# A list schedule with its own shift for each of 1150 pieces of work, 225 operations on another engine, and transfers modelled as loads and stores

## The chip, the cores and the metric

One core of a Trainium2 chip. The metric is the device time of one execution in microseconds (us); lower is better. The kernel before takes 780.31 us, the median of three runs (779.22 to 782.52).

## The reference

One layer of a streaming encoder on a sequence of 1024 rows and 1024 columns, all in fp32:

```python
h = rms_norm(x, norm_pre_g)
proj = h @ w_in                       # 1024 x 2976: sb_q, sb_k, sb_v, sb_g, c_q, c_kv, k_rope, mla_g
sb_o = stick_breaking_attention(...)  # 8 heads of 64: sigmoid and a suffix product over the past keys
sb_y = head_rms_norm(sb_o, ...) * silu(sb_g)
q    = rms_norm(c_q) @ w_uq           # 8 heads, low-rank q and kv, rotary part of 32
kv   = rms_norm(c_kv) @ w_ukv
mla_o = latent_attention(...)         # softmax over the visible chunks of 64
mla_y = head_rms_norm(mla_o, ...) * silu(mla_g)
y = concat(sb_y, mla_y) @ w_out
x = x + rms_norm(y, norm_post_g)
ple = rms_norm(p @ w_ple, ple_norm_g)
x = x + ple * sigmoid(x @ w_ple_gate + b_ple_gate)
```

## The kernel before

**Arithmetic.** A product of fp32 operands is made of three matmuls: each operand is split into a high part (`copy` to the type fp32r) and a low part (`tensor_tensor` subtract), and high x high, high x low and low x high are summed in PSUM. `split` makes the two parts; its `heng` and `leng` say on which engine. Tiles have 128 partitions and up to 512 columns; a PSUM bank is 128x512.

**Stages.** At the start the rows of `x` are loaded, normalised (`x_norm`), transposed on TensorE and split (`x_tr`), and multiplied by the columns of `w_in` for the values (`xv_gen`, 24 matmuls for each row tile). Then the two attentions run, 16 pairs (head pair, half of the queries), as `unit(i, s)`: load the head's queries and keys (`load_head`), scores and weights row block by row block (`sb_rows`, `mla_rows`), then transposes of the weights and the product with the values (`av`), then head norm and gate (`finish1` to `finish3`). Between them other projections are woven in as filler: queries and keys of later heads (`qk_gen`), the gates (`gate_gen`), the low-rank part (`c_gen`, `lr_*`), the per-layer embedding (`ple_gen`, around 400 to 480 us), and the output projection (`wo_gen`, `e1_gen`). The tail multiplies by `w_ple_gate` with a seven-product scheme (`wg_part`, `e2a`, `e2b`) and writes the output. Queries, keys, values, gates and other intermediate arrays go through DRAM (`q_d`, `k_d`, `v_d`, `gate_d`, `y_d`).

**What sets the order.** The program isn't issued as it is written. A `Recorder` takes every operation as a record with its dependences, a duration from `cost` and a priority; `schedule` then runs a list schedule over five queues (PE, ACT, DVE, POOL, and SP, which issues all transfers): of the operations that are ready on the queue that is free first, the one with the lowest priority number comes next. The priority is the number of the operation in the recorded order, plus `LOW` (336) for filler, minus `URGENT` or `AHEAD` in some places:

```python
prio=i + (LOW if self.low else 0) + self.bias
```

A tile of a pool gets its buffer in the recorded order of the tiles of that pool (`info["order"]`, `grant`): the pool `u` has 28 buffers for the main work, `f` has 10 for filler, PSUM has 3 banks `a` (sums of products) and 5 banks `t` (scores and transposes). `issue` then emits the operations sorted by their planned start, so every engine works through a fixed list. Since one line emits everything, all instructions have the same line in the profile (L517 here), and they are told apart by engine and by their tiles: `a` and `t` the PSUM banks, `u` and `f` the SBUF buffers, `h` the transposed input or later the large weights, names ending in `_d` DRAM arrays, names beginning with `in_` the inputs.

**Engines.** `choice(i)` puts the low part of a split or a product on DVE or POOL by the table `SPLITS`; high parts are on ACT or DVE by `heng`.

Of the kernel before, what the change touches and what calls it, by code (L numbers as in the profile page):

```python
# [52 lines left out]
LOW = 336  # L53
# [13 lines left out]
HEAD = ("v0", "x1", "x0", "g0", "v3", "v1", "v2", "x2")  # L67
AHEAD = 52
BANKS = {"a": ("a", 3), "t": ("t", 5), "s": ("t", 5), "v": ("a", 3), "l": ("t", 5)}


class Weaver:
# [13 lines left out]
    def _step(self):  # L86
        name, gen, low = self.queue[0]
        self.rec.low = low
# [5 lines left out]
        self.rec.low = False  # L94

    def spend(self, cost):
# [64 lines left out]
class Recorder:  # L161
# [3 lines left out]
    def __init__(self, nc):  # L165
        self.ins = []
        self.tiles = {}
        self.tags = {}
        self.access = {}
        self.low = False  # L170
        self.front = False
        self.bias = 0

        self.shadow = bacc.Bacc("TRN2", target_bir_lowering=False, num_devices=1)
        self.PE = Proxy(self, "PE", nc.tensor)
        self.ACT = Proxy(self, "ACT", nc.scalar)
        self.DVE = Proxy(self, "DVE", nc.vector)
        self.POOL = Proxy(self, "POOL", nc.gpsimd)
        self.SP = Proxy(self, "SP", nc.sync)

    def tile(self, pool, shape, dt, tag, slots, name, kind, part=None):
# [20 lines left out]
        return t  # L202

    def touch(self, ap, info):
# [10 lines left out]
    def add(self, eng, op, fn, args, kw):  # L215
        aps = [a for a in list(args) + [v for k, v in kw.items() if k != "accum_out"] if isinstance(a, bass.AP)]
        outs = [aps[0]]
        if kw.get("accum_out") is not None:
            outs.append(kw["accum_out"])
        i = len(self.ins)  # L220
        deps = {}
        uses = []
        spaces = []
        for is_w, group in ((False, aps[1:]), (True, outs)):
            for pos, ap in enumerate(group):
# [15 lines left out]
                else:  # L241
# [7 lines left out]
        func = kw.get("func", args[2] if len(args) > 2 and op == "activation" else None)  # L249
        self.ins.append(dict(port=port, eng=eng, op=op, fn=fn, args=args, kw=kw, deps=deps, uses=set(uses), dur=dur,  # L250
                             cols=self.columns(op, args) if eng == "PE" else 0,
                             prio=i + (LOW if self.low else 0) + self.bias, func=SETS.get(func) if op == "activation" else None))

# [11 lines left out]
    def cost(self, eng, op, args, kw, outs, aps, spaces):  # L265
        n = max(self.elems(a) for a in aps)
        ps = any(k == "psum" for _, k in spaces)
        if eng == "PE":
# [26 lines left out]
        run = min(self.run(a) for a in aps)  # L295
        total = self.elems(outs[0]) * outs[0].shape[0]
        return total / run * (7.0 + run * 4 * 0.0372) / 16 * 1.2

    def run(self, ap):
        info = self.tiles.get(ap.tensor.name)  # L300
        n = 1
        for stride, k in reversed(ap.ap[0 if info is None or info["kind"] == "dram" else 1:]):
# [9 lines left out]
           ("DVE", "POOL"): 156.0, ("DVE", "SP"): 120.0, ("POOL", "PE"): 180.0, ("POOL", "ACT"): 75.0,  # L312
           ("POOL", "DVE"): 65.0, ("POOL", "POOL"): 102.0, ("POOL", "SP"): 55.0, ("SP", "PE"): 1060.0,
           ("SP", "ACT"): 910.0, ("SP", "DVE"): 910.0, ("SP", "POOL"): 980.0, ("SP", "SP"): 910.0}

    def schedule(self):
        import heapq
        ins, LAT = self.ins, self.LAT
        n = len(ins)
        succ = [[] for _ in range(n)]  # L320
        need = [0] * n
# [24 lines left out]
        slot = {}  # L346
        dma_free = 0.0
        port_free = 0.0
        table = None
# [68 lines left out]
        while done < n:  # L418
# [101 lines left out]
def block_kernel(ctx, tc, x, p, positions, norm_pre_g, w_in, q_norm_g, w_uq, kv_norm_g, w_ukv,  # L520
# [245 lines left out]

    for item in HEAD:
        first(item)
    R.bias = -URGENT
    for n in range(2):  # L770
# [6 lines left out]
    x_norm(1)  # L777
    for t in range(4):
        for _ in xv_gen(t):
            pass  # L780
# [167 lines left out]
    def lr_load_gen():  # L948
        lr_load()
        yield 0.0  # L950

    for _ in qk0_gen(0):
        pass
    for dst, src in ((g_sb, sb_out_norm_g), (g_mla, mla_out_norm_g)):
# [255 lines left out]
    def unit(i, s):  # L1210
# [4 lines left out]
        g1 = sb_rows(i, s, rows) if c < 4 else mla_rows(i, s, rows, ess[c, s], e)  # L1215
        g2 = pending.pop(0) if pending else iter(())
        for cost in g1:
            yield cost
            run_later()
            for _ in range(s + 1):  # L1220
                yield next(g2, 0.0)
        yield from g2
        pending.append(av_unit(i, s, rows))
# [27 lines left out]
    def wg_part(i):  # L1251

        if i == 1:
            for nm in ("B11", "B21", "T1"):
                wg[nm] = []
            for k in range(4):
                raw, b12 = k4((128, 2, 512), F32, "wg_r"), k2(dt=F32, name="wg_b")
                SP.dma_start(raw, w2g[:, k::4, half[0]])
# [11 lines left out]
        for a, nm in enumerate((("T4", "T2") if i == 2 else ("T3", "B22"))):  # L1270
            wg[nm] = [(h_[:, k, a], l_[:, k, a]) for k in range(4)]
        for k in range(4):
            ra = k4((128, 2, 512), F32, "wg_r")
            SP.dma_start(ra, w2g[:, k::4, half[1]])
# [60 lines left out]
    def e2a(t):  # L1335
# [10 lines left out]
        def parts(nm, src, heng, leng):  # L1346
            h_, l_ = k2(name="ah"), k2(name="al")
            split(h_, l_, src, heng=heng, leng=leng)
            out_[nm] = (h_, l_)
        parts("A11", ps[0, 0], ACT, DVE)  # L1350
        f11, f21 = k2(dt=F32, name="f11"), k2(dt=F32, name="f21")
# [9 lines left out]
        DVE.tensor_tensor(s4, ps[0, 1], s2, ALU.subtract)  # L1361
        parts("S4", s4, ACT, choice(36))
        choice(37).tensor_tensor(f11, f11, f21, ALU.subtract)
        parts("S3", f11, ACT, choice(38))
# [17 lines left out]
    def e2b(t, order, last):  # L1382
# [19 lines left out]
        for i in order:  # L1402
            if i == 4 and last:
                for v in (slice(0, 256), slice(256, 512)):
                    close(1, 0, product(xs, 4, v), w, w, v, DVE)
                continue
            ps = product(xs, i)
            if i == 1:
# [40 lines left out]
    def prepare(u):  # L1449
# [10 lines left out]
        if u and c == 0 and s == 1:  # L1460
            weave.ensure("b1")
        load_head(i, s)

    prepare(0)
    for u, (i, s) in enumerate(units):
        load_v(i, s)
        if u + 1 < len(units):
# [8 lines left out]
    while pending:  # L1476
        for _ in pending.pop(0):
            pass
    for _ in range(5):
        run_later(True)  # L1480
    weave.drain()
    R.front = True
    for t in range(N1, 4):
        for _ in e1_gen(t):
            pass
    y_load(4)
    R.front = False
    weave.drain()
    firsts = 0
    for step in TAIL:  # L1490
        k, t = step[0], int(step[1])
        if k == "x":
# [11 lines left out]
        else:  # L1504
            R.front = True
            if t < 6:
                if t + 1 < NT:
                    y_load(t + 1)
                for _ in e1(t, True):
                    pass  # L1510
            else:
# [5 lines left out]
                for n in range(3):  # L1517
                    for g in both:
                        for cost in g:
                            if cost == 0.0:  # L1520
                                break
# [29 lines left out]
```

## Time and profile before

| | |
|---|---|
| median of three runs | 780.31 us (779.22 to 782.52) |
| the profiled execution | 780.85 us; span on the core 778.8 us |
| TensorE matmuls | 756.4 us busy (97%), 3912 instructions |
| VectorE (DVE) | 569.8 us (73%), 1041 |
| ScalarE (ACT) | 422.1 us (54%), 1001 |
| GpSimd (POOL) | 395.1 us (51%), 355 |
| DMA | 148.69 MB, mean 191 GB/s; 386 issues, all from SP |

Times in the profile are in us from the start of the span, durations of single instructions in ns. "PE" is TensorE's matmul, "PEld" its weight load, "SPq" the issue of a transfer. A row of the timeline gives start, length, engine, operation, tiles and, in brackets, the idle time of the engine before it and what ended that. Matmuls overlap in the pipeline, so their lengths don't add up; what counts for them is the distance from start to start.

### The profile page before, as it was taken

The numbers are of one execution on the slowest core, as the hardware profiler recorded it, in microseconds if no ns is written. First come the engines' busy times: TensorE is split into PE (matmuls) and PEld (weight loads), VectorE is DVE, ScalarE is ACT, GpSimd is POOL, SyncE is SP. The second block draws the span as 40 slices with busy tenths as digits, with TensorE's granted clock in tenths as the row PEclk, the third lists the DMA queues.
The fourth block names the chain that finished last, engine by engine and source line by source line (L and its number), as shares of the span: only waits on it lengthen the run. The fifth ranks groups of instructions, "written<-read, shape, count | busy, mean of one in ns | idle before, by whom it ended". The sixth has DMA issues, their size and how long they took to land.

```text
span 778.8 us, 11830 instructions
## 1 busy us (share of the span) xinstructions
PE 756.4 (97%) x3912; PEld 624.7 (80%) x3912; DVE 569.8 (73%) x1041; ACT 422.1 (54%) x1001; POOL 395.1 (51%) x355
## 2 busy tenths in 40 slices
PE   5999999999999999999999999999999999999996
PEld 3887879988888878888887787888888878878875
DVE  5784225389837869888997999987689879564755
ACT  5415224244526576667547676875967672444431
POOL 5654225102422258878877721323287025579975
PEclk9999999999999999999999999999999999999999
DMA  9544361168998636475455688597356377073331
GB/s 339 188 163 135 130 186 53 57 219 327 348 343 274 191 124 218 127 238 173 149 190 189 194 271 272 187 311 240 122 202 190 112 233 264 1 269 109 101 137 60
DMA packets 101966, 148.69 MB, mean 191 GB/s; under 512 B 7441, under 2 KB 55057, under 8 KB 101906
## 3 DMA queue, kind: packets, MB, share of 16 engines
q1 hardware_dynamic: 101906, 147.95, 56.7%
q8 instruction: 31, 0.51, 0.3%
q14 instruction: 29, 0.24, 0.1%
HBM read 101.26 MB, written 46.66 MB: 190 GB/s over the span
## 4 chain that ended last, share of the span: by engine, by line
PE 81%; DMA 6%; DVE 5%; POOL 4%; ACT 2%; issue 1%; SPq 1%; POOLq 0%; DVEq 0%; ACTq 0%
PE a L517 56%; PE t L517 24%; DVE u L517 3%; POOL u L517 2%; DMA u<-in_w_ple_gate_dram 2%; POOL h L517 1%; ACT u L517 1%; DMA u<-q_d 1%; DVE f L517 1%; DMA ple_d<-f 1%; DVE nm L517 1%; DMA q_d<-f 1%; DMA u<-in_norm_pre_g_dram 1%; SPq L517 1%; DMA f<-in_p_dram 1%
## 5 line engine op out<-in xcount | busy, mean ns | idle before, releaser
L517 POOL TENSOR_TENSOR u<-u,u 128x512 f32<-128x512 f32 (+18 forms) x171 | 241.1, 1426 | 116.9 <-DVE u L517 56.9
L517 PE MATMUL a<-h,f 128*128 128x512 f32 x864 | 241.0, 406 | 1.0 <-DVE f L517 0.8
L517 PEld LDWEIGHTS a<-h,f 128*128 128x128 f32 x864 | 155.8, 188 | 29.0 <-DVE f L517 1.5
L517 DVE TENSOR_TENSOR u<-t,u 128x512 fp32r<-128x512 f32 (+4 forms) x284 | 149.3, 555 | 29.6 <-ACT u L517 23.9
L517 PE MATMUL t<-u,u 128*128 128x512 f32 (+4 forms) x576 | 151.4, 368 | 1.0 <-DMA u<-q_d 0.9
L517 ACT CAST u<-t 128x512 fp32r<-128x512 f32 (+1 forms) x252 | 111.8, 490 | 65.0 <-PE t L517 46.2
L517 PE MATMUL a<-u,u 128*128 128x512 f32 (+2 forms) x522 | 133.1, 370 | 0.8 <-DVE f L517 0.3
L517 PE MATMUL t<-ident,u 128*128 128x128 f32 x792 | 125.3, 274 | 3.3 <-ACT u L517 1.7
L517 PEld LDWEIGHTS t<-u,u 128*128 128x128 f32 x576 | 103.0, 189 | 20.1 <-ACT u L517 2.8
L517 PEld LDWEIGHTS t<-ident,u 128*128 128x128 f32 x792 | 97.3, 141 | 23.1 <-ACT u L517 4.5
L517 ACT ACTIVATE u<-t 128x384 f32<-128x384 f32 (+5 forms) x208 | 91.2, 518 | 45.0 <-PE t L517 33.6
L517 PE MATMUL a<-h,u 128*128 128x512 f32 (+1 forms) x492 | 115.5, 390 | 0.0
L517 PEld LDWEIGHTS a<-u,u 128*128 128x128 f32 x522 | 92.8, 188 | 18.9 <-DVE u L517 1.3
L517 PEld LDWEIGHTS a<-h,u 128*128 128x128 f32 x492 | 90.5, 188 | 20.4
L517 DVE TENSOR_TENSOR_SCAN u<-u 128x64 f32<-128x64 f32 (+3 forms) x64 | 68.9, 1086 | 27.1 <-ACT u L517 24.3
L517 DVE TENSOR_TENSOR u<-a,u 64x512 f32<-64x512 f32 (+4 forms) x75 | 47.8, 651 | 40.6 <-PE a L517 18.5
L517 ACT ACTIVATE u<-t,nms 128x384 f32<-128x384 f32 (+4 forms) x96 | 55.1, 579 | 28.5 <-DVE nms L517 26.3
L517 ACT ACTIVATE f<-a 128x512 bf16<-128x512 f32 (+2 forms) x64 | 34.6, 542 | 59.0 <-PE a L517 58.2
L517 DVE TENSOR_TENSOR u<-u,u 128x512 fp32r<-128x512 f32 (+4 forms) x59 | 58.5, 1004 | 6.5 <-ACT u L517 3.6
L517 DVE TENSOR_TENSOR f<-a,f 128x512 f32<-128x512 f32 (+2 forms) x54 | 34.4, 644 | 32.9 <-ACT f L517 28.4
L517 POOL TENSOR_TENSOR u<-u 128x512 f32<-128x512 f32 (+8 forms) x34 | 39.4, 1173 | 35.7 <-ACT u L517 18.7
L517 DVE TENSOR_REDUCE nm<-t 128x1 f32<-128x384 f32 (+4 forms) x96 | 51.9, 547 | 3.5 <-PE t L517 2.7
(98 smaller groups left out, 768.3 us busy)
## 6 DMA issues: line engine op xcount, KB each, us to landing
u<-q_d SPq DMA_DIRECT2D x64, 256.0 KB, 4.5
u<-k_d SPq DMA_DIRECT2D x16, 512.0 KB, 6.2
u<-v_d SPq DMA_DIRECT2D x16, 512.0 KB, 5.5
u<-in_w_ple_gate_dram SPq DMA_DIRECT2D x16, 512.0 KB, 6.2
f<-in_w_in_dram SPq DMA_DIRECT2D x14, 512.0 KB, 4.3
v_d<-u SPq DMA_DIRECT2D x12, 512.0 KB, 3.4
f<-in_x_dram SPq DMA_DIRECT2D x9, 512.0 KB, 5.0
k_d<-u SPq DMA_DIRECT2D x9, 512.0 KB, 3.7
```

The source lines that it names most:

```text
L517: x["fn"](*[place(a) for a in x["args"]], **{k: place(a) for k, a in x["kw"].items()})
```

## The change

The list schedule, the operations recorded and their arithmetic stay. Four things change.

1. **A place of its own for each piece.** The recording is cut into 1146 numbered pieces (`piece`, called at each step of each generator). A table `SHIFT` gives a piece two numbers: the first is added to the priority of its operations, the second to the place of its tiles in the order in which buffers are handed out (`turn`). Pieces without an entry have no shift. The order of buffers is now sorted by this number.
2. **An engine of its own for 225 operations.** `FLIP` lists record numbers; `other` puts such an operation on the other engine: 126 copies from ACT to DVE (43 of them the high part of transposed attention weights, 128 to 512 columns out of PSUM), 23 copies from DVE to ACT, 58 two-operand products or differences from POOL to DVE (21 of them products of the stick-breaking weights), 18 from DVE to POOL. By engine: DVE 1041 to 1184 operations, ACT 831 to 728, POOL 349 to 309; PE and SP are unchanged.
3. **The planner's model of transfers.** A store is expected to start moving 0.5 us after its issue and a load 1.7 us after; descriptors in flight are limited to 1500; durations and the latencies after a transfer are other numbers.
4. **The planner's costs** of POOL operations and of matmuls on bf16 operands are other numbers.

```diff
+SHIFT = {
+    0: (-2123, -1458), 1: (-359, -1410), 2: (53, -217), 3: (-206, -329), 4: (46, -202), 5: (230, -104),
...
+FLIP = (
+    7, 13, 62, 88, 90, 108, 134, 144, 181, 183, 202, 234, 235, 264, 290, 307, 326, 386, 425, 432, 435, 438, 441, 444,
...
+            self.tiles[key].update(turn=self.turn(1), turn0=len(self.ins), chunk=self.chunk)
...
+    def turn(self, by=0):
+        return len(self.ins) + SHIFT.get(self.chunk, (0, 0))[by]
...
+        if i in FLIP:
+            eng, op, fn = self.other(eng, op)
...
-                             prio=i + (LOW if self.low else 0) + self.bias, func=SETS.get(func) if op == "activation" else None))
+                             chunk=self.chunk, prio=self.turn() + (LOW if self.low else 0) + self.bias, func=SETS.get(func) if op == "activation" else None))
+
+    def other(self, eng, op):
+
+        to = {("DVE", "tensor_tensor"): self.POOL, ("POOL", "tensor_tensor"): self.DVE,
+              ("ACT", "copy"): self.DVE, ("DVE", "tensor_copy"): self.ACT}[eng, op]
...
-                return max(60.0, n * 0.451)
+                return n * 0.305
...
-            return n * 2.105 + 148
...
+            ap = outs[0].ap
+            if int(ap[-1][0]) == 2:
+                return n * 2.76 + 107
+            return n * 1.76 + 135 if len(ap) > 2 and int(ap[-1][1]) == 2 else n * 2.217 + 84
...
+        for info in self.tags.values():
+            info["order"].sort(key=lambda key: self.tiles[key]["turn"])
...
-                free[e] = s + 430.0
-                dma_free = max(s + 1150.0, dma_free) + x["dur"]
+
+                while flight and flight[0][0] <= s:
+                    room -= heapq.heappop(flight)[1]
+                while flight and room + x["descs"] > 1500:
+                    t, k = heapq.heappop(flight)
+                    room -= k
+                    s = max(s, t)
+                free[e] = s + x["hold"]
+                dma_free = max(free[e] + x["lead"], dma_free) + x["dur"]
                 end = dma_free
+                heapq.heappush(flight, (end, x["descs"]))
+                room += x["descs"]
```

Nearly every row of every engine's list moves. Three places follow.

**The first transfers, on SP.** `u` buffers are filled from the weights `w_in`, from rows of `x`, and from the gain row `norm_pre_g`, which TensorE spreads over the partitions as its first work. Before, the gain row is fourth:

```order
L517 DMA u_0_115<-in_w_in_dram 128x2x512
L517 DMA u_3_121<-in_x_dram 128x1024
L517 DMA u_4_125<-in_x_dram 128x1024
L517 DMA u_6_127<-in_norm_pre_g_dram 1x1024
L517 DMA u_7_129<-in_w_in_dram 128x2x512
```

Now it is third, and the rows of `x` that come first are those that are transposed first:

```order
L730 DMA u_0_115<-in_w_in_dram 128x2x512
L730 DMA u_3_121<-in_x_dram 128x1024
L730 DMA u_12_125<-in_norm_pre_g_dram 1x1024
L730 DMA u_10_127<-in_x_dram 128x1024
L730 DMA u_7_129<-in_w_in_dram 128x2x512
```

The gain row has passed one row tile of `x`.

**The second head's queries, on SP, around 105 us.** `f` buffers hold query stores (to `q_d1`) and weights of the low-rank projection; `u` buffers receive the stored queries again. Before:

```order
L517 DMA f_4_924<-in_w_in_dram 128x2x416
L517 DMA q_d1_84<-f_3_931 256x1x512
L517 DMA u_23_957<-q_d1_84 128x512
L517 DMA u_23_957<-q_d1_84 128x1x512
L517 DMA u_18_970<-q_d1_84 128x512
L517 DMA u_18_970<-q_d1_84 128x1x512
L517 DMA f_0_979<-in_w_in_dram 128x2x416
L517 DMA q_d1_84<-f_7_965 256x1x512
```

Now:

```order
L730 DMA f_4_927<-in_w_in_dram 128x2x416
L730 DMA q_d1_84<-f_6_939 256x1x512
L730 DMA f_0_958<-in_w_in_dram 128x2x416
L730 DMA q_d1_84<-f_3_956 256x1x512
L730 DMA u_20_975<-q_d1_84 128x512
L730 DMA u_20_975<-q_d1_84 128x1x512
L730 DMA u_1_986<-q_d1_84 128x512
L730 DMA u_1_986<-q_d1_84 128x1x512
```

The last weights and the second half of the queries no longer stand behind the four loads, which wait for the first store.

**The first embedding tile, on ACT, around 411 us.** The copies (`CAST`) of a `t` bank of 256 columns to an `f` buffer are the high parts of the transposed embeddings; the `ACTIVATE` rows are the sigmoids of stick-breaking scores and one of a gate (from an `a` bank). Before:

```order
L517 ACTIVATE f_4_3268<-a_1_290 128x512
L517 ACTIVATE u_23_3894<-t_1_180 128x512
L517 ACTIVATE u_8_3902<-t_1_180 128x512
L517 ACTIVATE u_23_3894<-t_4_249 128x512
L517 ACTIVATE u_8_3902<-t_4_249 128x512
L517 CAST f_0_3914<-t_0_164 128x256
L517 CAST f_0_3914<-t_3_198 128x256
L517 CAST u_27_3867<-t_4_249 128x128
```

Now:

```order
L730 ACTIVATE f_4_3481<-a_1_325 128x512
L730 CAST f_1_3894<-t_3_184 128x256
L730 CAST f_1_3894<-t_1_157 128x256
L730 ACTIVATE u_5_3901<-t_2_176 128x512
L730 ACTIVATE u_17_3909<-t_2_176 128x512
L730 ACTIVATE u_5_3901<-t_0_151 128x512
L730 ACTIVATE u_17_3909<-t_0_151 128x512
```

The two copies have passed the four sigmoids.

More of the change, by code (lines that the diff above doesn't have):

```diff
@@ L87, in _step @@
         name, gen, low = self.queue[0]
+        outer = self.rec.thread
+        self.rec.piece(name)
         self.rec.low = low
@@ L94, in _step @@
         self.rec.low = False
+        self.rec.piece(outer)
     def spend(self, cost):
@@ L249, in add @@
         func = kw.get("func", args[2] if len(args) > 2 and op == "activation" else None)
-        self.ins.append(dict(port=port, eng=eng, op=op, fn=fn, args=args, kw=kw, deps=deps, uses=set(uses), dur=dur,
+        back = any(int(st) < 0 for a in aps for st, _ in a.ap)
+        stored = eng == "SP" and spaces[-1][1] != "sbuf"
+        self.ins.append(dict(port=port, hold=525.0 if back else 420.0, descs=self.descriptors(aps, outs) if eng == "SP" else 0, lead=500.0 if stored else 1700.0, eng=eng, op=op, fn=fn, args=args, kw=kw, deps=deps, uses=set(uses), dur=dur,
                              cols=self.columns(op, args) if eng == "PE" else 0,
-                             prio=i + (LOW if self.low else 0) + self.bias, func=SETS.get(func) if op == "activation" else None))
+                             chunk=self.chunk, prio=self.turn() + (LOW if self.low else 0) + self.bias, func=SETS.get(func) if op == "activation" else None))
+    def other(self, eng, op):
+        to = {("DVE", "tensor_tensor"): self.POOL, ("POOL", "tensor_tensor"): self.DVE,
+              ("ACT", "copy"): self.DVE, ("DVE", "tensor_copy"): self.ACT}[eng, op]
+        op = {"copy": "tensor_copy", "tensor_copy": "copy"}.get(op, op)
+        return to.name, op, getattr(to.eng, op)
     def columns(self, op, args):
@@ L312 @@
            ("DVE", "POOL"): 156.0, ("DVE", "SP"): 120.0, ("POOL", "PE"): 180.0, ("POOL", "ACT"): 75.0,
-           ("POOL", "DVE"): 65.0, ("POOL", "POOL"): 102.0, ("POOL", "SP"): 55.0, ("SP", "PE"): 1060.0,
-           ("SP", "ACT"): 910.0, ("SP", "DVE"): 910.0, ("SP", "POOL"): 980.0, ("SP", "SP"): 910.0}
+           ("POOL", "DVE"): 65.0, ("POOL", "POOL"): 102.0, ("POOL", "SP"): 55.0, ("SP", "PE"): 650.0,
+           ("SP", "ACT"): 620.0, ("SP", "DVE"): 620.0, ("SP", "POOL"): 650.0, ("SP", "SP"): 620.0}
     def schedule(self):
@@ L767, in block_kernel @@
     for item in HEAD:
+        R.piece(item)
         first(item)
+    R.piece("head")
     R.bias = -URGENT
@@ L778, in block_kernel @@
     for t in range(4):
+        R.piece("xv")
         for _ in xv_gen(t):
@@ L950, in lr_load_gen @@
         yield 0.0
+    R.piece("qk0")
     for _ in qk0_gen(0):
-        pass
+        R.piece("qk0")
     for dst, src in ((g_sb, sb_out_norm_g), (g_mla, mla_out_norm_g)):
@@ L1216, in unit @@
         g2 = pending.pop(0) if pending else iter(())
+        th = f"u{c}{e}{s}"
+        R.piece(th)
         for cost in g1:
             yield cost
+            R.piece("later")
             run_later()
             for _ in range(s + 1):
+                R.piece(th + "v")
                 yield next(g2, 0.0)
-        yield from g2
+            R.piece(th)
+        for cost in g2:
+            yield cost
+            R.piece(th + "v")
         pending.append(av_unit(i, s, rows))
@@ L1256, in wg_part @@
             for k in range(4):
+                R.piece("w1")
                 raw, b12 = k4((128, 2, 512), F32, "wg_r"), k2(dt=F32, name="wg_b")
@@ L1272, in wg_part @@
         for k in range(4):
+            R.piece(f"w{i}")
             ra = k4((128, 2, 512), F32, "wg_r")
@@ L1349, in parts @@
             out_[nm] = (h_, l_)
+        R.piece(f"a{t}")
         parts("A11", ps[0, 0], ACT, DVE)
@@ L1362, in e2a @@
         parts("S4", s4, ACT, choice(36))
+        R.piece(f"a{t}")
         choice(37).tensor_tensor(f11, f11, f21, ALU.subtract)
@@ L1461, in prepare @@
             weave.ensure("b1")
+        R.piece("load")
         load_head(i, s)
@@ L1465, in block_kernel @@
     for u, (i, s) in enumerate(units):
+        R.piece("loadv")
         load_v(i, s)
@@ L1477, in block_kernel @@
         for _ in pending.pop(0):
-            pass
+            R.piece("lastv")
+    R.piece("later")
     for _ in range(5):
@@ L1483, in block_kernel @@
     for t in range(N1, 4):
+        R.piece(f"e1{t}")
         for _ in e1_gen(t):
-            pass
+            R.piece(f"e1{t}")
+    R.piece("y4")
     y_load(4)
@@ L1490, in block_kernel @@
     for step in TAIL:
+        R.piece(step)
         k, t = step[0], int(step[1])
@@ L1509, in block_kernel @@
                 for _ in e1(t, True):
-                    pass
+                    R.piece(step)
             else:
@@ L1519, in block_kernel @@
                         for cost in g:
+                            R.piece(step)
                             if cost == 0.0:
```

19 lines of the change are left out of this document (16 added, 3 removed), and 161 rows, old and new, of tables (FLIP, SHIFT).

## Prediction

> **What bounds the kernel now.** I read the page first, then the waits of TensorE, then the timeline at each of them, then busy time by stretches of 20 us, and the groups of instructions for prices.
>
> ```profile
> span 778.8 us, 11830 instructions
> PE 756.4 (97%) x3912; PEld 624.7 (80%) x3912; DVE 569.8 (73%) x1041; ACT 422.1 (54%) x1001; POOL 395.1 (51%) x355
> GB/s 339 188 163 135 130 186 53 57 219 327 348 343 274 191 124 218 127 238 173 149 190 189 194 271 272 187 311 240 122 202 190 112 233 264 1 269 109 101 137 60
> ```
>
> TensorE bounds the kernel from end to end. No matmul is removed or added, so a new order can only take away time in which TensorE does nothing. The span less its busy time is 778.8 - 756.4 = 22.4 us, and its waits say where most of that lies:
>
> ```profile
> PE t L517 <- DMA u<-in_norm_pre_g_dram: 7.1, 1, 7.1
> PE t L517 <- ACT u L517: 1.7, 2, 1.2
> PE t L517 <- DVE u L517: 1.6, 2, 0.9
> PE a L517 <- ACT f L517: 1.2, 2, 0.8
> PE a L517 <- DMA u<-q_d: 1.2, 1, 1.2
> PE a L517 <- DVE f L517: 1.1, 2, 0.8
> PE t L517 <- DMA u<-q_d: 0.9, 2, 0.5
> PE a L517 <- DVE h L517: 0.8, 1, 0.8
> ```
>
> (Columns: total us, times, longest.) 7.1 us are the wait for the first operand. The 12 waits below it make 8.5 us, and the rest lies after the last matmul. Each wait costs a little more than its idle time, since the pipeline has to fill again. To see that, take the pace without a wait and one wait:
>
> ```profile
> 30.77 5.82 PE L517 MATMUL a<-u,h 128*128 128x512 f32 x24
> 36.43 1.03 PE L517 MATMUL t<-ident,u 128*128 128x128 f32 x8
> ```
>
> 24 matmuls of 512 columns go from 30.77 to 36.43, 0.236 us each from start to start. Eight transposes last 1.03 us and four, in the next rows, 0.60: 0.11 for each more.
>
> ```profile
> 411.81 2.06 ACT L517 ACTIVATE u<-t 128x512 f32<-128x512 f32 x4
> 412.18 0.60 PE L517 MATMUL t<-ident,f 128*128 128x128 f32 x4
> 413.93 0.33 PE L517 MATMUL t<-ident,u 128*128 128x128 f32 x1 [1.15 <-ACT u L517]
> ```
>
> Four transposes from 412.18 would let the next work start at 412.62. It starts at 413.93: 1.31 us lost where 1.15 is shown. So I add 0.2 us to each wait (0.16 here). The 12 waits are then worth 8.5 + 12 x 0.2 = 10.9 us. That, something at the start, and something after the last matmul are the most that the rows show to be had, out of 778.8.
>
> **The change part by part.** Each part is a place; the sum goes against the profiled execution, 780.85 us.
>
> *Start.* The first work of TensorE spreads the gain row; then come a scaling on DVE, transposes, and the first products.
>
> ```profile
> 2.21 0.34 SPq L517 DMA_DIRECT2D u<-in_norm_pre_g_dram  x1
> 7.13 3.75 PE L517 MATMUL t<-u,ones 1*128 1x512 f32 x4 [7.13 <-DMA u<-in_norm_pre_g_dram]
> 15.28 1.22 PE L517 MATMUL a<-u,h 128*128 128x512 f32 x2 [0.76 <-DVE h L517]
> ```
>
> The gain row is issued fourth, at 2.21, and used at 7.13. It passes one issue (about 0.5 us) and one 512 KB transfer, which at the 339 GB/s of the first slice is 1.5 us. So TensorE starts 0.5 to 2.0 us earlier. What of that reaches the first product depends on the sums of squares of `x`, on ACT and POOL, which do not get faster; I take 0.8. Then, before 15.28, TensorE waits for the low part that DVE makes. In the new list eight transposes of the next row tile (8 x 0.11 = 0.9 us) stand in that wait, so 0.8 of it goes. Together -1.6; the ends are 0 (the row is hidden behind the squares, and the wait moves on) and -3.0.
>
> *The first head's scores, 63.6 us.*
>
> ```profile
> 63.64 0.39 PE L517 MATMUL t<-u,u 128*128 128x256 f32 x1 [0.40 <-DMA u<-q_d]
> ```
>
> They wait for queries on their way back from DRAM. In the new list two transposes and five products of 512 columns, which stood behind them, stand ahead: 2 x 0.11 + 5 x 0.236 = 1.4 us of work against a wait of 0.40 + 0.2. -0.6; ends 0 and -0.6. Behind the waiting scores nothing else is queued that is late.
>
> *The second head's scores, 112 to 117 us.*
>
> ```profile
> 112.47 1.95 POOL L517 TENSOR_TENSOR f<-f,f 128x832 fp32r<-128x832 f32 x1 [12.74 <-DVE f L517]
> 112.59 0.73 PE L517 MATMUL a<-f,h 128*128 128x416 f32 x3
> 114.48 0.64 PE L517 MATMUL a<-f,h 128*128 128x416 f32 x2 [1.16 <-DMA u<-q_d]
> 116.60 0.69 PE L517 MATMUL t<-u,u 128*128 128x256 f32 x3 [0.45 <-DMA u<-q_d]
> ```
>
> The row at 114.48 names the queries, but these matmuls read `f` and `h`: they wait for the low part of the weights, which POOL finishes at 114.42. The change moves that operation to DVE. It also puts 18 matmuls of another row tile, which need only weights that are there, ahead of these, at about 0.19 each (112.59 and its two successors) 3.4 us of work. The four query loads on SP now stand behind one weight load and one store, which I count as 1 us later; the 3.4 us cover it. Of 1.16 + 0.45 + 2 x 0.2 = 2.0 I take -1.8; ends 0 (the loads come later than the work lasts) and -2.0.
>
> *The embedding, 412 to 480 us.* The waits for ACT `u`, ACT `f` and DVE `f` above, 1.7 + 1.2 + 1.1 = 4.0 us in six waits, all lie here; with 6 x 0.2 that is 5.2. In the first one ACT works through four sigmoids (411.81, 2.06 us) while two short copies wait behind them that would free TensorE's next operand; now the copies come first, and the four sigmoids, which DVE's scan needs, come two copies later. Not all are mended:
>
> ```profile
> 444.68 1.98 PE L517 MATMUL a<-f,f 128*128 128x512 f32 x6 [0.40 <-ACT f L517]
> ```
>
> Here the new list still has the product right behind the transposes it depends on, so this wait stays, 0.6, and I leave 0.3 for the rest. -4.3; ends 0 and -5.2.
>
> *The last head, 637 us.*
>
> ```profile
> 637.45 0.66 PE L517 MATMUL t<-ident,u 128*128 128x128 f32 x4 [0.94 <-DVE u L517]
> ```
>
> DVE's operation waited for a copy on ACT that stood behind a large weight copy; it is now ahead of it. -1.0; ends 0 and -1.1.
>
> *After the last matmul.*
>
> ```profile
> 767.62 5.33 PE L517 MATMUL a<-h,u 128*128 128x512 f32 x34
> 772.48 1.26 DVE L517 TENSOR_TENSOR u<-u,u 128x256 f32<-128x256 f32 x1 [0.48 <-ACT u L517]
> 774.00 1.94 DVE L517 TENSOR_TENSOR u<-u,u 128x256 f32<-128x256 f32 x3
> ```
>
> The last matmul ends at 772.95 and the last product on DVE at 775.94. One product of 256 columns took 1.26 us; three took 1.94. Two POOL products of 512 columns lay beside them, and in the new list these two are DVE's, while one short one is POOL's. I take the slow one's excess, -0.7; ends +0.6 (DVE has two more in its queue) and -1.0.
>
> *The 225 operations.* The prices are:
>
> ```profile
> L517 ACT CAST u<-t 128x512 fp32r<-128x512 f32 x124 | 69.7, 599 | 47.8 <-PE t L517 36.9 <-POOL u L517 3.7 <-DMA q_d<-u 1.8
> L517 DVE TENSOR_TENSOR u<-t,u 128x512 fp32r<-128x512 f32 x124 | 81.8, 680 | 15.8 <-ACT u L517 15.1
> L517 DVE TENSOR_TENSOR u<-u,u 128x512 f32<-128x512 f32 x16 | 18.1, 1128 | 2.5 <-DMA u<-in_w_ple_gate_dram 1.7 <-DMA out_dram<-u 0.5
> L517 POOL TENSOR_TENSOR u<-u,u 128x512 f32<-128x512 f32 x54 | 81.1, 1511 | 59.4 <-DVE u L517 45.4 <-ACT u L517 12.6 <-DMA u<-gate_d 1.0
> ```
>
> The trace has no full-width copy out of PSUM on DVE. Its nearest row is the subtraction that reads the same bank, 680 ns; the lower end is ACT's 599. The net of 103 copies at 0.6 to 0.68, many narrower than 512 (I take 0.5 on the mean), is some 52 us; the net of 40 products at 0.68 to 1.13 is 27 to 45. DVE thus gains 80 to 97 us, to 650 to 667 of 770 (85%); I take 86, or 2.2 for each of 39 stretches of 20 us. Beside TensorE that is free wherever DVE has 2.2 us left. The fullest stretches:
>
> ```profile
> 160.00:180.00 20.00, 20.00 (x90) 15.98 (x88) 18.92 (x37) 10.28 (x25) 0.00 (x0) 1.00 0.69 259
> 180.00:200.00 20.00, 20.00 (x89) 16.15 (x88) 19.31 (x29) 8.99 (x16) 6.38 (x8) 1.00 0.86 326
> 380.00:400.00 20.00, 20.00 (x108) 16.50 (x107) 19.19 (x20) 11.42 (x27) 14.72 (x11) 1.00 0.70 220
> 460.00:480.00 20.00, 18.66 (x104) 15.55 (x102) 19.51 (x54) 14.00 (x41) 4.34 (x6) 1.00 0.79 246
> 480.00:500.00 20.00, 20.00 (x119) 17.44 (x119) 18.94 (x45) 14.28 (x38) 3.79 (x5) 1.00 0.79 276
> ```
>
> (The third busy number is DVE's.) Five stretches have 4.1 us left in all and would get 11: 6.9 too much, if it fell evenly and nothing could slide. Since TensorE stood only 1.3 us in 460 to 480 with DVE at 19.51, full DVE is not yet a stall, and I take +0.7; ends 0 and +6.9.
>
> [...]
>
> Sum: -1.6 - 0.6 - 1.8 - 4.3 - 1.0 - 0.7 + 0.7 = -9.3, so 771.55 for such an execution. The profiled one is 0.54 above the median of 780.31, so the median comes out at 771.0.
>
> **The rivals.**
>
> *More goes than the rows show.* Waits shorter than the pipeline's fill leave no idle time in the trace. If all 10.9 us of waits go, 3.0 at the start, 1.0 at the end, and nothing is paid on DVE, the gain is 14.9: 765.4. For it: every piece has a shift of its own. Against it: the wait at 444.68 stays, and a fixed list can't follow an engine that is 0.2 us late.
>
> *The waits move on.* The lists are fixed, every row of them is new, and each wait removed makes another operand the latest. If half of the gain comes back as new waits, -4.6: 775.7; if all does, 780.3. I put this case at 778. For it: the embedding's stretches are short of ACT and DVE at once.
>
> *DVE becomes the bound (slower).* The place is 160 to 200 and 380 to 500. The price is 5 times the addition per stretch less 4.1 us; with 3.2 instead of 2.2 us it is 11.9. The gains outside 412 to 480 are 5.7, so the time is 780.3 + 11.9 - 5.7 = 786.5. It decides from an addition of 2.7 us in each, where the loss passes these gains by 3.9. [...]
>
> **How the numbers follow.** The forecast (768 to 775) has 0.56, the larger gain (764 to 768) 0.20, the waits that move on (775 to 782) 0.17, DVE as the bound 0.06, below 764 0.01. A measurement of this kernel can tell 0.5%, 3.9 us, from no change: faster is below 776.4. Faster: 0.56 + 0.20 + 0.01 and 0.03 of the third, 0.80. Within: 0.13. Slower: 0.06 and 0.01 of the third, 0.07. The range from 764 to 778 leaves out 0.01 below, and above it 0.06 and some 0.10 of the third. It is 771.0 less 7.0 (the far ends of all parts, 3.6, and the rest for waits that do not show) and plus 7.0 (DVE's upper end alone, 6.2 more).
>
> **What the profile after would show.** The gain row used before 6.7 instead of 7.13; no wait for `q_d` on TensorE at 63 and 114; the six waits between 412 and 480 down to about 1 us; TensorE's busy time near 755 in a span near 769.5; DVE 640 to 670, ACT near 370, POOL near 340. The forecast is wrong if new waits for DVE appear on TensorE around 160 to 200 or 380 to 500, if TensorE's idle time is more than 18 us, or if the first products start no earlier than 13.

## The result, and the profile after

The changed kernel takes 774.54 us (median of 774.4, 774.54, 775.21, 775.29 and 774.52) against 780.31: a ratio of 0.9924, 95% interval 0.9898 to 0.9949. Run again in another set it took 775.03, ratio 0.9928 (0.9914 to 0.9942). So it is 5.8 us faster, where 9.3 were forecast.

The page of the profile after, the rows that answer to those of before:

```profile
span 772.6 us, 11778 instructions
PE 754.5 (98%) x3912; PEld 621.5 (80%) x3912; DVE 624.1 (81%) x1184; ACT 384.9 (50%) x898; POOL 346.6 (45%) x315
```

TensorE is idle for 772.6 - 754.5 = 18.1 us instead of 22.4. DVE is busy 54 us longer, ACT 37 and POOL 49 shorter. The waits of TensorE (total us, times, longest):

```profile
PE t L730 <- DMA u<-in_norm_pre_g_dram: 6.0, 1, 6.0
PE t L730 <- DVE u L730: 2.8, 5, 1.2
PE a L730 <- DVE u L730: 0.9, 2, 0.5
PE a L730 <- DVE f L730: 0.6, 1, 0.6
PE t L730 <- DVE f L730: 0.6, 2, 0.3
PE t L730 <- DMA u<-q_d: 0.5, 1, 0.5
PE t L730 <- ACT u L730: 0.3, 1, 0.3
PE a L730 <- ACT f L730: 0.3, 1, 0.3
PE t L730 <- DMA u<-k_d: 0.3, 1, 0.3
```

Those for ACT fell from 2.9 to 0.6 us; those for DVE rose from 3.5 to 4.9, in ten instead of five places. The queue has moved to another engine.

Idle time shows only part of what is lost, so I added up, over all 3912 matmuls, the time from one start to the next less the pace of that shape without a wait (0.232 us for 512 columns, 0.11 for a transpose). At these paces the matmuls take 736.3 us in each profile; the rest of the span is lost time:

| stretch, us | forecast | before | after | after, second profile |
|---|---|---|---|---|
| 0 to 20 (first wait, cold pace) | -1.6 | 12.6 | 9.7 | 8.8 |
| 60 to 80 | -0.6 | 1.8 | 1.6 | 1.3 |
| 100 to 120 | -1.8 | 2.5 | 1.5 | 2.0 |
| 120 to 160 | | 0.5 | 2.0 | 1.8 |
| 160 to 400 | | 4.8 | 7.5 | 9.0 |
| 400 to 480 | -4.3 | 8.1 | 5.1 | 5.1 |
| 620 to 640 | -1.0 | 1.4 | 0.3 | 0.3 |
| after the last matmul | -0.7 | 5.9 | 5.2 | 5.2 |
| all else | | 4.8 | 3.4 | 4.7 |
| sum | -10.0 | 42.4 | 36.2 | 38.2 |

("Cold pace" is the slower pace of the first matmuls, 0.427 us for 512 columns and 0.213 for a transpose.) In the first profile the six places of the forecast gave 9 of the 10.0 us forecast for them. Between 120 and 400 us, for which the forecast had no term of its own and +0.7 for DVE's load everywhere, 4.2 us were lost anew (5.5 in the second profile).

### The profile page after: what moved, and what is told of

It reads as the page before. It is cut to its first block, busy times and chain, and to the rows that moved or that the text cites. A ratio compares the mean times of both kernels' runs of the same rounds, so it can differ in the third digit from the quotient of the medians.

```text
span 772.6 us, 11778 instructions
## 1 busy us (share of the span) xinstructions
PE 754.5 (98%) x3912; PEld 621.5 (80%) x3912; DVE 624.1 (81%) x1184; ACT 384.9 (50%) x898; POOL 346.6 (45%) x315
## 4 chain that ended last, share of the span: by engine, by line
PE 84%; DVE 7%; DMA 4%; ACT 2%; issue 1%; POOL 1%; SPq 1%; POOLq 0%; ACTq 0%; DVEq 0%
PE a L730 58%; PE t L730 26%; DVE u L730 4%; DVE f L730 2%; ACT u L730 1%; DMA u<-k_d 1%; DMA u<-in_w_ple_gate_dram 1%; DMA u<-q_d 1%; DMA u<-in_x_dram 1%; DMA f<-in_positions_dram 1%; DMA q_d<-f 1%; SPq L730 1%; DVE nm L730 1%; ACT f L730 0%; POOL u L730 0%
## 5 line engine op out<-in xcount | busy, mean ns | idle before, releaser
L730 POOL TENSOR_TENSOR u<-u,u 128x512 f32<-128x512 f32 (+16 forms) x134 | 200.5, 1512 | 153.3 <-DVE u L730 64.0
L730 PE MATMUL t<-u,u 128*128 128x512 f32 (+4 forms) x580 | 154.4, 370 | 1.9 <-DMA u<-q_d 0.5
L730 PE MATMUL a<-u,u 128*128 128x512 f32 (+2 forms) x524 | 136.7, 371 | 0.5 <-DVE u L730 0.5
L730 ACT ACTIVATE u<-t 128x512 f32<-128x512 f32 (+5 forms) x208 | 91.0, 509 | 67.7 <-PE t L730 57.8
L730 ACT CAST u<-t 128x512 fp32r<-128x512 f32 (+3 forms) x187 | 85.6, 495 | 71.0 <-PE t L730 35.3
L730 PEld LDWEIGHTS a<-u,u 128*128 128x128 f32 x524 | 93.1, 188 | 17.2 <-DVE u L730 2.2
L730 DVE TENSOR_TENSOR_SCAN u<-u 128x64 f32<-128x64 f32 (+6 forms) x64 | 59.1, 934 | 20.6 <-ACT u L730 20.4
L730 DVE TENSOR_TENSOR u<-u,u 128x512 f32<-128x512 f32 (+13 forms) x91 | 73.2, 820 | 2.0 <-ACT u L730 1.1
L730 POOL TENSOR_TENSOR rs<-ms,nhalf 128x8 f32<-128x8 f32 x16 | 27.7, 1731 | 57.0 <-DVE ms L730 37.5
L730 ACT ACTIVATE f<-a 128x512 bf16<-128x512 f32 (+3 forms) x64 | 34.3, 538 | 36.7 <-PE a L730 32.1
L730 PE MATMUL a<-u,h 128*128 128x512 f32 x192 | 49.8, 406 | 0.0
```

What stands on the lines that cost most here:

```text
L730: x["fn"](*[place(a) for a in x["args"]], **{k: place(a) for k, a in x["kw"].items()})
```

## The experiments

Three questions: is the gain in the order, in the engines, or in the planner's new prices; why does it stop at 5.8 us; and are the new waits local, so that they can be mended one by one?

**Order alone, engines alone, prices alone.** The first kernel is the changed one with its own planned lists, but just ahead of the issue each of the 225 operations is given back, at its place in the list, to the engine it had in the kernel before. The second does the reverse to the kernel before: its lists stay, and only the engines of the 225 change. The third empties both tables.

```diff
+            for i in SWAP:
+                x = self.ins[i]
+                x["eng"], x["op"], x["fn"] = self.other(x["eng"], x["op"])
             for i in order:
                 x = self.ins[i]
```

> The changed kernel with its lists as planned, but each of the 225 operations given back, at the same place of the list, to the engine it had before. Theory A (the gain is the order; the 225 operations only load DVE, and 2.2 us of TensorE's new waits are waits for DVE): 772 to 775 us, DVE busy near 570, TensorE's waits for DVE down from 4.9 to below 3 us. Theory B (order and engines belong together; the list is only good with the engine it was laid for): 778 us or more, with new waits of TensorE for ACT and POOL, ACT busy near 420, POOL near 395.

> The kernel before with its lists, and only the 225 operations moved to the other engine, each at its old place in time. Theory A (the gain is the order): 780 to 784 us, no wait of the kernel before is removed, and DVE's 85 us more bring some new ones between 160 and 200 and between 380 and 500. Rival E (relief of ACT and POOL is itself the gain): 774 to 777 us. Theory B (both belong together): 782 us or more.

> The changed kernel with both tables empty: only the new prices of POOL and of the bf16 products, the new transfers and the order of buffers by turn are left. Rival C (the better prices and transfers alone give it): 774 to 776 us. Theories A and B (the tables give it): 778 to 783 us, with waits of TensorE of 8 us or more below the first one, as before.

Measured: order alone 795.0 us (ratio 1.0168, 1.0137 to 1.0199), engines alone 815.58 (1.0428, 1.0397 to 1.0459), prices alone 798.9 (1.0227, 1.0196 to 1.0258). Theory A, mine, falls: neither the order nor the engines give anything by themselves, and each alone costs more than the two together bring. Theory B holds for these two. Rivals C and E fall too. That the prices alone cost 17 us (798.9 beside 781.73), no theory expected: theories A and B had 778 to 783 for it.

The first rows of TensorE's waits of the engines alone, without the one for the gain row:

```profile
PE t L539 <- DVE u L539: 8.9, 12, 1.8
...
PE a L539 <- DVE u L539: 6.4, 10, 1.7
PE t L539 <- ACT u L539: 5.9, 10, 1.2
```

Relief did not help ACT's customers: a copy that goes to DVE at its old place stands behind whatever DVE has there. Each engine works through its list in order, and an operation that is not ready holds up what follows it (in the third set below a copy on DVE, ahead of an operation of 0.69 us, begins only after 2.55 us of idle time).

**Which of the 225: products or copies?** The same, for the 76 products or the 149 copies only.

> The changed kernel with its lists as planned, but only the 76 products (58 of DVE's, 18 of POOL's) given back at their places; the copies stay moved. All 225 given back cost 20.5 us. Theory L (the products carry it, since a POOL product beside a DVE operation with two operands in SBUF makes the latter longer): 785 to 795 us, DVE's scans at a mean of 1.0 us or more instead of 0.93, POOL busy near 385. Theory K (the copies carry it, since they free ACT's list): 775 to 780.

> The changed kernel with its lists as planned, but only the 149 copies (126 of DVE's, 23 of ACT's) given back at their places; the products stay moved. Theory L (the products carry the 20.5 us): 775 to 780 us, DVE busy near 570. Theory K (the copies carry it): 785 to 795 us, with TensorE's new waits for ACT, whose copies stand behind its exponentials again.

Measured: products given back 794.17 us (1.0177, 1.0149 to 1.0205), copies given back 785.39 (1.0073, 1.0045 to 1.01). Above the changed kernel the products cost about 19.6 us and the copies 10.9, both together 20.5: the two do not add up. Theory L got its time for the products and theory K its time for the copies, so neither is the whole; and L's mechanism is not what happened: with the products back, DVE's scans did not become longer.

```profile
L517 DVE TENSOR_TENSOR_SCAN u<-u 128x64 f32<-128x64 f32 (+3 forms) x64 | 68.9, 1086 | 27.1 <-ACT u L517 24.3
```

```profile
L730 DVE TENSOR_TENSOR_SCAN u<-u 128x64 f32<-128x64 f32 (+6 forms) x64 | 59.1, 934 | 20.6 <-ACT u L730 20.4
```

```profile
L737 DVE TENSOR_TENSOR_SCAN u<-u 128x64 f32<-128x64 f32 (+6 forms) x64 | 59.7, 942 | 27.0 <-ACT u L737 26.6
```

(Groups of DVE instructions by line: before, after, products given back. Behind the first bar stand the busy time in us and the mean of one in ns.) The mean falls from 1086 to 934 ns with the change and stays at 942 with the products back on POOL; in the engines alone, where POOL has as few products as in the changed kernel, it is 1085. So it isn't the number of POOL's products that makes the scans shorter, but where in time they lie beside them. What the products cost lies then, I take it, in the place they fill in POOL's list, which was laid without them; no row shows that by itself.

**The tables one at a time, with new lists.** Here the planner lays the lists anew, without `FLIP` or without `SHIFT`.

> The changed kernel with the shifts of the pieces and the new prices, without the 225 operations on other engines; the planner lays the lists anew. The lists with all 225 given back afterwards cost 795.0, since the list was laid for the other engines. If the shifts are good by themselves, a list laid anew gives 774 to 780; if shifts and engines were fitted to each other, it gives 785 to 800, like the kernel with both tables empty (798.9) or little better.

> The changed kernel with the 225 operations on other engines and the new prices, without the shifts of the pieces; the planner lays the lists anew. If the relief of ACT and POOL is good by itself: below the 798.9 us of both tables empty by 10 us or more (785 to 789). If shifts and engines were fitted to each other: 795 to 810.

Measured: without the engines 808.39 us (1.0334, 1.0309 to 1.0359), without the shifts 809.76 (1.0369, 1.0352 to 1.0385). Each table alone is worse than neither (798.9). So the two tables belong to each other; with the new prices they are worth, by the ratios, 1.0227 - 0.9924 or 23.6 us, of which 17.7 only make good what the new prices cost without them.

**Are the waits local? First set.** Seven moves in the final lists of the changed kernel and two operations on other engines, at four places; nothing else moves.

```diff
+SWAP = (8, 3603)
+BEHIND = ((11, 2), (43, 25), (44, 30), (45, 44), (16, 46), (3038, 3075), (3700, 3708))
...
+            for i, j in BEHIND:
+                order.remove(i)
+                order.insert(order.index(j) + 1, i)
```

> The changed kernel with seven moves in its lists and two operations moved to another engine, aimed at four waits. Start: the gain row's transfer goes first (1.7 to about 0.8), the low part of the first weights moves from POOL to DVE (POOL then makes the root 0.5 earlier), its scaling stands ahead of the second tile's mean on DVE and the gain's copies ahead of the second squares on ACT: the fifth transpose at 10.4 instead of 11.41, -1.0. The wait at 426.64 (1.18 for DVE): the product of 384 columns at 424.59 goes back to POOL, which is idle there, -0.55. The wait at 381.43: the combination of 0.70 us that frees the bank goes ahead of one of 1.74, -0.5. The wait at 437.31: one of 0.66 ahead of a scan of 1.76, -0.4. If waits are local (theory A): 774.5 - 2.4 = 772.1. If every wait only moves on to the next operand (theory M): 774 to 775, with waits of like size a few us further on.

Measured: 774.43 us (0.9911, 0.988 to 0.9943), no difference from the changed kernel that can be told. Start and 381 went as expected or better: the fifth transpose at 10.30 instead of 11.41, and at 383 every matmul 0.8 us further ahead of its time in the changed kernel than at 380. The other two went wrong. At 426 the timeline of the changed kernel reads:

```profile
424.59 0.55 DVE L730 TENSOR_TENSOR u<-u,u 128x384 f32<-128x384 f32 x1
...
425.05 0.95 DVE L730 TENSOR_TENSOR_SCAN u<-u 128x384 f32<-128x384 f32 x1
...
425.92 1.26 DVE L730 TENSOR_TENSOR u<-t,u 128x512 fp32r<-128x512 f32 x2
...
426.64 0.66 PE L730 MATMUL t<-ident,u 128*128 128x128 f32 x4 [1.18 <-DVE u L730]
```

and with the product back on POOL:

```profile
422.53 1.19 POOL L738 TENSOR_TENSOR u<-u,u 128x384 f32<-128x384 f32 x1 [1.56 <-ACT u L738]
422.70 1.83 DVE L738 TENSOR_TENSOR_SCAN u<-u 128x384 f32<-128x384 f32 x1
...
424.46 1.26 DVE L738 TENSOR_TENSOR u<-t,u 128x512 fp32r<-128x512 f32 x2
...
425.18 0.66 PE L738 MATMUL t<-ident,u 128*128 128x128 f32 x4 [1.59 <-DVE u L738]
```

DVE's list became 0.55 us shorter, and the same scan, now begun 0.17 us behind a POOL product of 1.19, took 1.83 us instead of 0.95. The wait grew from 1.18 to 1.59. At 437 the wait went, but the next DVE operation behind the moved scan, of 128x1, now took 1.24 us beside a POOL product instead of 0.61; DVE's scale factor, for which ACT and then TensorE wait at 440, came 1.34 us earlier than in the changed kernel, TensorE 2.2 us earlier, and that wait grew from 0.32 to 1.15. Theory M holds at these two places and theory A at the other two.

**Second and third set.** Kept are the start and 381; new are a reduction moved at 424 and the transfer of the gate's bias, first; then an operation more moved to DVE at 111.

```diff
+SWAP = (8,)
+BEHIND = ((11, 2), (43, 25), (44, 30), (45, 44), (16, 46), (3038, 3075), (3565, 3625), (5927, 5935), (5915, 5967), (5916, 5915), (5917, 5916))
```

> The changed kernel with moves in the lists that bring no new pair of a POOL product and a DVE operation with two operands in SBUF side by side. Kept from the first set: the start (measured there: 1.8 us of TensorE's time before 20) and the combination ahead of the long one at 381 (0.8). Left out: the two moves behind which the next wait grew (the product of 384 columns on POOL, which made DVE's scan 1.83 instead of 0.95 us; the scan behind another operation, which made the wait at 440 longer). New: a reduction of 0.68 us, not needed soon, goes behind two evictions at 424 (-0.4 at 426.64), and the transfer of the gate's bias goes ahead of one weight load on SP, with two short DVE operations behind the two sums that use it (-0.5 at 690.44). If the waits are local: 774.5 - 1.8 - 0.8 - 0.4 - 0.5 = 771.0. If what is gained is taken back by the next wait, as in the first set (theory M): 773 to 775.

> The changed kernel once more, to stand on the same chip and beside the same runs as the next one: 773.5 to 776 us, and the same waits as in its first profile within 0.1 us, since its lists are fixed.

The third set is the second without `(3565, 3625)` and with `SWAP = (8, 757)`.

> The changed kernel with only those moves that gave time in the two sets before: the start, the combination at 381, the gate's bias at 690; and one operation more given to another engine: the high part of the compressed keys' weights, 0.89 us on ACT before the low part's 1.03 on DVE, goes to DVE (0.56 by its width), which is idle there. Waits local: -0.9 (start), -0.8, -0.6, and -0.33 at 112.69, so 2.6 us below the changed kernel run beside it, 771.9. Theory M (taken back by the next waits): less than 1 us below it.

Measured: second set 772.58 us (0.9907, 0.988 to 0.9934). By the ratios that is 1.3 us below the changed kernel, where 3.5 were expected, and the two intervals overlap, so no gain can be told. In its profile, beside the first one of the changed kernel, 381 (0.8) and 690 (0.6) gave what they should. The start gave 0.9 where 1.8 were expected: in the first set's profile eight transposes in the cold pace had taken 1.40 us, here 1.91 as in the changed kernel. The move at 424 gave 0.2 at 426.64 and took 0.4 at 428.5 and 0.2 at 437.3. Third set 774.98 (0.9922, 0.9908 to 0.9936) beside 775.03 of the changed kernel: nothing, where 2.6 were expected. Its profile names the reason:

```profile
110.93 0.59 DVE L738 CAST f<-f 128x832 fp32r<-128x832 f32 x1 [2.55 <-DMA q_d<-f]
111.56 0.69 DVE L738 TENSOR_TENSOR u<-a,u 64x512 f32<-64x512 f32 x1
...
112.28 1.02 DVE L738 TENSOR_TENSOR f<-f,f 128x832 fp32r<-128x832 f32 x1
...
113.36 0.46 PE L738 MATMUL a<-f,h 128*128 128x416 f32 x1 [1.33 <-DVE f L738]
```

The copy at 110.93 could not begin earlier, whichever engine had it (110.69 on ACT in the changed kernel). On DVE, idle or not, it now held up the operation of 0.69 us behind it, which then stood between the copy and the subtraction that TensorE waits for. I had read DVE's idle time there as free; it was free only for an operation that is ready.

The longer wait (1.33 us instead of 0.60) was not the whole price. Behind it, from 114 to 116, the granted clock (third number from the right) was one half:

```profile
114.00:116.00 2.00, 2.00 (x8) 1.90 (x7) 0.00 (x0) 0.12 (x1) 1.80 (x1) 0.50 0.94 270
```

The matmuls of 416 columns there start 0.347 us apart instead of 0.19. Between 100 and 120 this kernel lost 4.0 us, the changed kernel 1.5 and 2.0 in its two profiles. The difference is about what the other moves had given.

The second profile of the changed kernel is as telling. Its waits for DVE and ACT at 112, 382, 427, 438 and 443 are the same as in the first within 0.02 us, but three others are not (timeline of the second profile, then the rows of the first):

```profile
111.04 0.46 PE L730 MATMUL a<-f,h 128*128 128x416 f32 x1 [0.50 <-ACT f L730]
...
219.66 0.50 PE L730 MATMUL t<-u,u 128*128 128x512 f32 x1 [1.88 <-DMA u<-k_d]
...
692.42 0.47 PE L730 MATMUL a<-h,u 128*128 128x512 f32 x1 [1.36 <-DVE u L730]
```

```profile
111.63 0.46 PE L730 MATMUL a<-f,h 128*128 128x416 f32 x1
...
218.70 0.50 PE L730 MATMUL t<-u,u 128*128 128x512 f32 x1 [0.26 <-DMA u<-k_d]
...
690.44 0.47 PE L730 MATMUL a<-h,u 128*128 128x512 f32 x1 [0.40 <-DVE u L730]
```

All three hang on a transfer: at 111 the copy on ACT waited for a store of queries (1.78 us there, 1.33 in the first profile); at 219 a load of keys stands behind another load, which landed 2.3 us after the store before it in the first profile and 4.1 in the second; at 690 it is the gate's bias. My expectation of the same waits within 0.1 us missed here.

**A version that beats both.** The moves that had given time in each profile that had them, and the long load ahead of 219 put behind the loads that are needed first.

```diff
+SWAP = (8,)
+BEHIND = ((11, 2), (43, 25), (44, 30), (45, 44), (16, 46), (3038, 3075), (5927, 5935), (5915, 5967), (5916, 5915), (5917, 5916), (1735, 1660))
```

> The changed kernel with the moves whose gain came back in each profile that had them (the start, -0.9; the combination at 381, -0.8; the gate's bias at 690, -0.6 to -1.5), without the operation given to DVE at 111 (it stood blocked on its queue and held up two others), and with one transfer moved: a load of 2.3 us in the first profile and 4.1 in the second, not used before 224, goes behind the loads that the scores at 219 wait for (-0.4 to -2.0). Waits local: the changed kernel's ratio to the kernel before, 0.9924 and 0.9928 in two sets, falls by 2.7 to 4.8 us, to 0.987 to 0.989. Theory M (taken back by the next waits): 0.991 to 0.993.

Measured: 772.04 us, ratio 0.9881 (0.9859 to 0.9903); as expected (0.987 to 0.989). The interval lies below that of the changed kernel's second set (0.9914 to 0.9942) and overlaps that of its first (0.9898 to 0.9949), but each of its six runs (770.76 to 772.87) is below each of the changed kernel's ten (774.4 to 776.43). Beside the first profile of the changed kernel the same matmuls come 1.2 us earlier by 20 us, 0.8 more at 381 and 0.6 more at 690. At 219 they gain 0.4, as in the second set without the transfer moved, so what that move is worth is not shown. At 381 the cause is plain. In the changed kernel a DVE operation with both operands in SBUF stands between TensorE and the one that frees its bank, and takes 1.74 us beside a POOL product:

```profile
377.69 2.42 POOL L730 TENSOR_TENSOR f<-f,f 128x1024 fp32r<-128x1024 f32 x1
...
378.91 1.74 DVE L730 TENSOR_TENSOR u<-u,u 128x512 fp32r<-128x512 f32 x1
...
380.68 0.69 DVE L730 TENSOR_TENSOR u<-a,u 64x512 f32<-64x512 f32 x1
...
381.43 2.13 PE L730 MATMUL a<-u,u 128*128 128x512 f32 x8 [0.55 <-DVE u L730]
```

With the two DVE operations exchanged, the long one meets only the last 0.30 us of the product and takes 0.84, and TensorE does not wait:

```profile
376.77 2.40 POOL L738 TENSOR_TENSOR f<-f,f 128x1024 fp32r<-128x1024 f32 x1
...
378.87 0.84 DVE L738 TENSOR_TENSOR u<-u,u 128x512 fp32r<-128x512 f32 x1
...
379.79 1.54 PE L738 MATMUL a<-u,u 128*128 128x512 f32 x6
```

## Why the prediction was right and where it failed

- **Start, -1.6: more came, -2.9.**

```profile
5.99 3.75 PE L730 MATMUL t<-u,ones 1*128 1x512 f32 x4 [5.99 <-DMA u<-in_norm_pre_g_dram]
10.51 1.97 PE L730 MATMUL t<-ident,u 128*128 128x128 f32 x8 [0.77 <-DVE u L730]
12.29 1.22 PE L730 MATMUL a<-u,h 128*128 128x512 f32 x2
```

  The gain row went third, TensorE began at 5.99 instead of 7.13 (forecast: before 6.7), and the first transposes at 10.51 instead of 11.51: 1.0 where I took 0.8. The wait before 15.28 is filled by transposes, as read from the order, 1.2 with its refill; the first products begin at 12.29. The other 0.7 lie in the cold pace, which I had not counted and which is not the same in each profile (-3.8 in the second). Putting the row first, with the moves behind it, brought the first transposes forward by another 0.9 to 1.2 us in four profiles.
- **First head, -0.6: -0.2.** The wait did not go: TensorE comes there some 1.5 us earlier and waits 0.54 us at 62.14 for the same queries. The 1.4 us of work ahead of it were used up by that.
- **Second head, -1.8: -1.0.** The wait for the queries went; the one for the low part of the weights, now a DVE operation behind an ACT copy, is the new last one, 0.60 at 112.69. (-0.5 in the second profile, with the added wait at 111.)
- **Embedding, -4.3: -3.0.** The two copies passed the sigmoids and the wait at 413.93 is gone. Its place is taken by 426.64, for DVE.
- **Last head, -1.0, and the end, -0.7: -1.1 and -0.7.** Right, by their own steps.
- **The 225 operations, +0.7, and nothing for any other new wait: this step failed.** I priced the operations as load on DVE in its fullest stretches, and put waits that the new lists make elsewhere at nothing. Matching each operation in the two traces by its place in the recording, the 184 operations that came to DVE took 119.9 us and the 41 that left had taken 34.1: 86 net, as forecast. But the 1000 that stayed became 17.2 us shorter (9.7 of it the scans, 6.6 the two-operand operations on `u` buffers), for which the forecast's sum had no term, and successive DVE instructions that overlap do so by 0.08 us, 860 times instead of 695, so busy time rose by 54 only. And the fullest stretches, 160 to 200, did not stall (0.2 us more lost there in the first profile), with DVE as full as before:

```profile
180.00:200.00 20.00, 20.00 (x88) 15.97 (x87) 19.76 (x31) 8.07 (x14) 5.85 (x6) 1.00 0.93 344
```

  The cost came where DVE had room. TensorE's waits between 120 and 400, of which the kernel before has none:

```profile
PE a L730 <- DVE u L730: 0.5, 1, 0.5
PE t L730 <- DVE u L730: 0.4, 2, 0.2
PE t L730 <- DVE f L730: 0.3, 1, 0.3
PE t L730 <- DMA u<-k_d: 0.3, 1, 0.3
```

  By the distance from start to start, seven matmuls that wait for DVE (137.21, 151.47, 155.54, 157.34, 254.46, 376.64 and 381.43) lose 2.9 us, and the one that waits for keys 0.4; in the kernel before, all that is lost behind DVE there is 0.3. Outside that stretch 426.64 and 437.31 are of the same kind and took back part of the embedding's gain. Busy time was the wrong measure; what counts on an engine that is a server for TensorE is what stands ahead of the one operation that is waited for. And only at 151.47 and 254.46 is one of the 225 among the four operations just ahead of that one, at 381.43 none: so these waits show first of all in the new order of DVE's list. How much of them the 225 cause from further back is open.
- **Of the rivals,** the waits that move on is what happened in part: half of the gain given back would be 775.7, 1.2 us off, while the 778 at which I put this case is as far off (3.5) as the forecast's 771.0. That the time still lies inside the forecast's 768 to 775, by 0.5 (the second set's 775.03 lies just outside), owes something to luck: the start gave 1.3 more than its term, which paid for part of what was left out. DVE as the bound did not come. That the order removes waits no row shows did not come either ("all else" gave 1.4 in the first profile, 0.1 in the second).
- **What I took for granted and the runs refuted:** that order and engines can be priced one by one. The forecast's sum came near since it took both from the new lists together.
- **Of the signs named,** ACT at 385 and POOL at 347 are near the 370 and 340 forecast, DVE at 624 is below 640. New waits for DVE on TensorE between 380 and 500, and more than 18 us of idle time (18.1), were to show the forecast wrong, and they show it in size. The wait for the queries near 63 was to go and stayed, and the waits between 400 and 480 came to 2.2 us, not about 1.

Not settled: what the remaining 0.9 or so of the 4.2 us are, and which of the small waits between 120 and 400 could be mended; only 381 was seen to go at its place (0.8 us in each of four profiles).

## What to carry to other kernels

A fixed list per engine and the choice of engines are one design: changing the engines of the 225 operations at their old places cost 34 us here (815.58 beside 781.73), and the whole change gained 6. Before moving an operation to an engine that looks idle, look whether it is ready there and what stands behind it, and which POOL product would run beside it. And look at a wait in two profiles of the same kernel before mending it: of those compared here, five between engines repeat within 0.02 us, and three behind transfers moved by 0.5 to 1.6.

## What the hardware showed

- **A DVE scan that began during a POOL product took longer.** 1.83 us instead of 0.95, above. The changed kernel's first profile has eight scans of 128x384. Three meet no POOL product that began before them and took 0.95 us. Four began with 0.41, 1.04, 1.14 and 1.23 us of a product still to come and took 1.22, 1.85, 1.95 and 2.05: the rest of the product and 0.81. One began with 0.13 to come and took 0.95. One of the first three began 0.27 us ahead of a product; there the scan is not longer, but the product is, 1.66 us where the one of the same shape at 422.53 in the first set, which began ahead of its scan, took 1.19:

```profile
317.03 0.95 DVE L730 TENSOR_TENSOR_SCAN u<-u 128x384 f32<-128x384 f32 x1
317.30 1.66 POOL L730 TENSOR_TENSOR u<-u,u 128x384 f32<-128x384 f32 x1 [1.78 <-ACT u L730]
```

- **After long waits TensorE's pace fell too.** In the order alone, one wait of 3.29 us for the queries is followed, 2.3 us later, by matmuls of 512 columns that start 0.427 us apart instead of 0.232; six of them in the row at 67.13, and the granted clock of 60 to 80 is 0.91:

```profile
64.86 0.38 PE L745 MATMUL t<-u,u 128*128 128x256 f32 x1 [3.29 <-DMA u<-q_d]
...
67.13 3.44 PE L745 MATMUL a<-u,h 128*128 128x512 f32 x9
```

  In the third set, one half from 114 to 116 followed waits of 0.44 and 1.33 us. Without the shifts, several waits of 0.2 to 1.9 us close together came with 0.74 to 0.83 in three stretches of 20 us, where 8.0, 9.3 and 6.9 us were lost with TensorE idle for 3.7 to 3.9. So these variants, whose lists don't fit, lost more than their idle time shows. One wait of 3.29 us came ahead of the slower clock, and so did shorter ones close together; from which length on a wait brings it is not shown.
- **The start varied with the clock.** The same eight transposes took 1.91 us at 13.31 in one profile of the changed kernel and 1.25 at 13.37 in the other; the trace's record of the full clock begins at 15.78 in the one and at 13.79 in the other. By 20 us the second is 0.9 us ahead, as much as the moves at the start gave.
